# One more entry in a placer's table: a transfer that depends on an earlier transfer of the same queue

## Chip, cores and metric

One core of one Trainium2 chip. The metric is the device time of one execution of the whole program in microseconds (us).

## What is computed

One layer of a hybrid backbone: 512 latent tokens and a prefix of 256 context tokens, model width 2048. A conditioning vector makes shift, scale and gate; the normalised tokens go through one input projection (`u = h @ w_in`, 8 kinds of 1024 columns each and some gate columns); half of the columns feed a bidirectional gated DeltaNet with 8 heads of 128, the other half a bidirectional RWKV-7 with 16 heads of 64; both branches are normalised, gated, and go through one output projection and a final RMSNorm. The part that matters here is the chunk of 64 tokens:

```python
lmat = jnp.where(strict, jnp.einsum('bhncd,bhnsd->bhncs', kb, k) * decay, 0.0)
tmat = lax.linalg.triangular_solve(eye + lmat, jnp.broadcast_to(eye, lmat.shape),
                                   left_side=True, lower=True, unit_diagonal=True)
u = tmat @ (v * beta[..., None])
wk = tmat @ (kb * jnp.exp(g)[..., None])
...
def step(state, inp):
    u_i, wk_i, attn_i, q_i, k_i, gl_i = inp
    v_new = u_i - wk_i @ state
    o_i = q_i @ state + attn_i @ v_new
    state = state * jnp.exp(gl_i)[..., None, None] + jnp.einsum('bhcd,bhce->bhde', k_i, v_new)
    return state, o_i
```

Every chunk of every head needs the inverse of a unit triangular 64x64 matrix before the scan over chunks can start.

## The kernel before

**Stages.** The work is cut into 16 mixers. Mixers 0 to 7 are the context mixers (one DeltaNet head and two RWKV heads each, 256 tokens); mixers 8 to 15 are the latent mixers (512 tokens), which start from the states that the context mixers left. The front stage (to about 150 us) makes the normalised tokens. In the context stage TensorE runs the input projection of kinds `Gk`, `Gv`, `Rk`, `Rv` for both token sets, and the context mixers run beside it. Then come the other projections (512 latent tokens alone) beside latent mixers 8 to 10, which share one set of buffers (a lane); latent mixers 11 to 15 alternate between two lanes, beside the four passes of the output projection. Weights come as 128x512 pieces: a load `wr`, a rounding to `wh` on ScalarE, a remainder `wl` on VectorE, and then three products per 128x128 block (`accl<-hhi,wh`, `hlo,wh`, `hhi,wl`; with the context columns also three on `accc`).

**A mixer.** `prep_*` and `blocks` fill the tile `Z` (`Z<-br`). `send` (line 976) stores the 32x32 diagonal blocks of `Z` into the DRAM buffer `DA` with eight transfers. `solve` (line 985) loads `DA` into `solNL`, inverts all blocks at once with 60 short VectorE operations (`solT<-solNL`, `solNL<-solNL,solT`) and stores the result and its transpose into the DRAM buffer `DD`. `levels` (line 1005) loads `DD` back, with four transfers into `lt` and eight into `Z`, and puts the 32x32 blocks together to 64x64 with two bundles of small products (`wm<-lt,Z` and `pss<-Z,lt`). `chain` (line 1044) is the scan over chunks, `outp` the gated normalisation. So each mixer holds two places where a transfer reads what an earlier one wrote: `DA` (store, then load) and `DD` (store, then loads). All transfers are issued by SP, in the order in which the program lists them.

PSUM tiles have in the trace the name of the first tile in their slot: `wm`, `pss` and `br` are work banks, `accl` and `accc` accumulators of the projections. `Gk` and `t` stand for several SBUF tiles of one slot, `gw` and `ks` are GpSimd's inputs (the gate weights, and the sums behind a key's norm).

**What sets the order.** The kernel records all operations (`record`, line 352), and a list scheduler, the placer (`schedule`, line 450), sets in which order each engine gets them; line 705 issues them, so nearly every row of the profile shows that line. The placer keeps a clock per engine and gives each engine the operation that is ready and of the highest rank. An operation becomes ready when its predecessors are done, plus a latency from two tables: `LAT` for two engines, `OWN` for one (line 396), with -1 where nothing is to be waited for:

```python
            if a.eng == eng:
                lat = OWN.get(eng, -1) if sync else -1
...
                c.ready = max(c.ready, (s if lat < 0 else fin + lat))
```

With -1 the dependent may be placed from the predecessor's start `s`, else from its end `fin`. For a transfer, `s` is the start of its issue on SP, and the placer's `fin` is its own idea of the landing (475 ns of issue, 650 ns, the bytes over 360 per ns, 900 ns). The order only: the real waits are semaphores, and are there whatever the placer thinks. Where the placer sees TensorE without work it puts in fill products (`wm<-zero`).

Of the kernel before, what the change touches and what calls it, by code (L numbers as in the profile page):

```python
# [85 lines left out]
def layout(inp):  # L86
# [22 lines left out]
    def put(n, a):  # L109
# [36 lines left out]
LAT = {"VV": 127, "VA": 128, "VG": 155, "VT": 149, "VS": 110, "AV": 142, "AA": 140, "AG": 125, "AT": 164, "AS": 110,  # L146
       "GG": 97, "GV": 60, "GA": 75, "GT": 120, "GS": 110, "TV": 196, "TA": 197, "TG": 224, "TS": 200,
       "ST": 2000, "SV": 600, "SA": 600, "SG": 600}
OWN = {"V": 120, "A": 148, "G": 107}
EXTRA = {"V": 93, "A": 70, "G": 48, "T": 50, "S": 50, "P": 0}  # L150
HAM, WARM = 10240 / 3, 3060

# [128 lines left out]
class Rec:  # L281
# [70 lines left out]
    def record(self, eng, fn, args, kw):  # L352
# [41 lines left out]
        for a, sync in preds.items():  # L394
            if a.eng == eng:
                lat = OWN.get(eng, -1) if sync else -1
            else:
# [1544 lines left out]
```

## Time and profile before

| | |
|---|---|
| time, median of 3 runs | 2160.66 us (2158.78 to 2163.45) |
| the profiled execution | 2166.2 us, its span 2164.4 us |
| TensorE busy | 1966.3 us (91%) |
| VectorE busy | 1475.2 us (68%) |
| ScalarE, GpSimd busy | 815.9 us (38%), 640.2 us (30%) |

The span is from the first to the last instruction; 1.8 us of the profiled execution's time lie around it. TensorE's busy share is no measure of its useful work: products overlap, their ends are modelled, and fill products count.

### The profile page before, as it was taken

What the parts mean: (1) busy time and instruction counts of PE and PEld (TensorE: products, weight loads), DVE (VectorE), ACT (ScalarE), POOL (GpSimd) and SP (SyncE); (2) the same over time, 40 slices, a digit from 0 to 9 for tenths busy, and PEclk for the clock granted to TensorE, in tenths of its full rate; (3) what the DMA queues carried; (4) which work ended last, traced back from release to release, by engine and by line L of the source; (5) the groups of instructions that cost most, each with busy time, mean ns of one, the idle gap of its engine ahead of it and who ended that gap; (6) DMA issues with size and microseconds to landing.
All of it is one profiled execution on the core that took longest, in us unless ns stands there. A gap on an engine that the chain in (4) does not pass through costs nothing.

```text
span 2164.4 us, 44432 instructions
## 1 busy us (share of the span) xinstructions
PE 1966.3 (91%) x16999; PEld 1542.0 (71%) x17000; DVE 1475.2 (68%) x3397; ACT 815.9 (38%) x2127; POOL 640.2 (30%) x799
## 2 busy tenths in 40 slices
PE   7999999999999999999999999978887897889877
PEld 5678887777877778776777777756665666667666
DVE  6436578675867769574765865786868577767747
ACT  4443333333242433324434434436424452435235
POOL 0003404213140421101212202235823564246226
PEclk8999999999999999999999999999979899899998
DMA  8964433333333333344541542544631544044702
GB/s 305 358 221 109 114 92 95 94 89 88 95 98 90 103 101 88 84 114 124 143 133 47 157 128 67 177 140 143 202 87 44 150 154 136 24 123 123 229 12 97
DMA packets 230517, 269.33 MB, mean 124 GB/s; under 512 B 117280, under 2 KB 130080, under 8 KB 226208
## 3 DMA queue, kind: packets, MB, share of 16 engines
q1 hardware_dynamic: 230304, 266.49, 41.8%
q8 instruction: 133, 2.18, 0.4%
q14 instruction: 80, 0.66, 0.1%
HBM read 210.50 MB, written 55.89 MB: 123 GB/s over the span
## 4 chain that ended last, share of the span: by engine, by line
PE 51%; DVE 22%; DMA 12%; issue 5%; SPq 5%; ACT 3%; POOL 3%; DVEq 0%; ACTq 0%; POOLq 0%
PE accl L705 23%; PE wm L705 8%; PE pss L705 7%; PE br L705 7%; PE accc L705 6%; DVE solNL L705 6%; SPq L705 5%; DVE solT L705 4%; DMA DD<-solNL 3%; DVE Gk L705 3%; DVE wl L705 2%; DMA DA<-Z 1%; DVE t L705 1%; DMA solNL<-DA 1%; DMA yl<-yd 1%
## 5 line engine op out<-in xcount | busy, mean ns | idle before, releaser
L705 ACT ACTIVATE wh<-wr 128x512 fp32r<-128x512 f32 x312 | 196.1, 629 | 375.5 <-PE accc L705 144.3
L705 PE MATMUL accl<-hhi,wl 128*128 128x512 f32 x768 | 317.1, 413 | 10.9 <-DVE wl L705 10.9
L705 PE MATMUL accl<-hhi,wh 128*128 128x512 f32 x768 | 314.1, 409 | 1.8 <-issue 1.8
L705 PE MATMUL accl<-hlo,wh 128*128 128x512 f32 x768 | 312.7, 407 | 0.0
L705 DVE TENSOR_TENSOR wl<-wr,wh 128x512 fp32r<-128x512 f32 x264 | 187.6, 713 | 106.9 <-ACT wh L705 102.5
L705 PE MATMUL accl<-yh,wh 128*128 128x512 f32 x480 | 199.3, 418 | 22.0 <-ACT yh L705 13.8
L705 PE MATMUL accl<-yl,wh 128*128 128x512 f32 x480 | 198.7, 414 | 0.1
L705 PE MATMUL accl<-yh,wl 128*128 128x512 f32 x480 | 197.1, 412 | 1.5 <-DVE wl L705 0.9
L705 PEld LDWEIGHTS accl<-hhi,wl 128*128 128x128 f32 x768 | 146.9, 191 | 50.9 <-DVE wl L705 13.3
L705 DVE TENSOR_TENSOR solNL<-solNL,solT 48x30 f32<-48x30 f32 (+29 forms) x480 | 175.2, 365 | 10.3
L705 DVE TENSOR_TENSOR solT<-solNL 48x30 f32<-48x30 f32 (+29 forms) x480 | 170.6, 355 | 9.0
L705 POOL TENSOR_TENSOR SRd<-Sbd,Dd 64x128 f32<-64x128 f32 x160 | 71.1, 444 | 354.2 <-DVE Sbd L705 348.1
L705 PE MATMUL wm<-zero 128*128 128x128 bf16 x1846 | 146.2, 232 | 30.3 <-DVE SG L705 15.0
L705 PEld LDWEIGHTS accl<-hhi,wh 128*128 128x128 f32 x768 | 146.9, 191 | 20.6 <-issue 4.3
L705 PEld LDWEIGHTS accl<-hlo,wh 128*128 128x128 f32 x768 | 147.0, 191 | 20.2 <-issue 3.2
L705 PEld LDWEIGHTS <-zero 128*128 128x128 bf16 x1864 | 124.4, 105 | 51.7 <-issue 46.6
L705 PE MATMUL accc<-clo,wh 128*128 128x256 f32 x512 | 149.9, 293 | 0.0
L705 PE MATMUL accc<-chi,wh 128*128 128x256 f32 x512 | 147.6, 288 | 0.0
L705 PE MATMUL accc<-chi,wl 128*128 128x256 f32 x512 | 145.9, 285 | 0.0
L705 PEld LDWEIGHTS accl<-yh,wh 128*128 128x128 f32 x480 | 90.9, 191 | 43.2 <-ACT yh L705 15.0
L705 PEld LDWEIGHTS accc<-clo,wh 128*128 128x128 f32 x512 | 97.3, 190 | 24.1 <-issue 0.9
L705 PEld LDWEIGHTS accc<-chi,wh 128*128 128x128 f32 x512 | 97.3, 190 | 21.5 <-issue 0.7
(312 smaller groups left out, 4207.8 us busy)
## 6 DMA issues: line engine op xcount, KB each, us to landing
wr<-win SPq DMA_DIRECT2D x256, 256.0 KB, 3.2
wa<-wada SPq DMA_DIRECT2D x32, 1024.0 KB, 6.0
ud<-Gk SPq DMA_DIRECT2D x72, 256.0 KB, 2.6
gw<-wada SPq DMA_DIRECT2D x64, 256.0 KB, 3.5
wr<-wout SPq DMA_DIRECT2D x64, 256.0 KB, 2.9
Rk<-ud SPq DMA_DIRECT2D x48, 256.0 KB, 3.2
rtd<-xt SPq DMA_DIRECT2D x48, 256.0 KB, 2.2
xr<-rtd SPq DMA_DIRECT2D x32, 256.0 KB, 3.0
```

The lines of the kernel that those rows point to most:

```text
L705: r = getattr(self.engs[o.eng], o.fn)(*args, **kw)
```

## The change

`OWN` gets an entry for transfers. A transfer that depends on an earlier one is now ready 1500 ns after the placer's landing of the earlier one, and no longer at the start of its issue. Nothing else is edited; no operation, tile or buffer is added or removed, apart from the fill products that the placer puts in itself.

```diff
 LAT = {"VV": 127, "VA": 128, "VG": 155, "VT": 149, "VS": 110, "AV": 142, "AA": 140, "AG": 125, "AT": 164, "AS": 110,
        "GG": 97, "GV": 60, "GA": 75, "GT": 120, "GS": 110, "TV": 196, "TA": 197, "TG": 224, "TS": 200,
        "ST": 2000, "SV": 600, "SA": 600, "SG": 600}
-OWN = {"V": 120, "A": 148, "G": 107}
+OWN = {"V": 120, "A": 148, "G": 107, "S": 1500}
```

The order of all engines changes. On SP, around the second context mixer's second hop, before:

```order
L705 DMA wr_0_1430<-win 128x512
L705 DMA DD_1_116<-solNL_1424 48x2x1024
L705 DMA lt_0_2052<-DD_1_116 32x6x32
L705 DMA Z_1_2025<-DD_1_116 32x6x32 x2
...
L705 DMA ud_110<-Gk_1_1443 128x512
L705 DMA wr_1_1431<-win 128x512
L705 DMA wr_2_1432<-win 128x512
L705 DMA gw_0_1453<-wada 128x512
L705 DMA gw_2_1455<-wada 128x512
```

and now:

```order
L705 DMA wr_1_1431<-win 128x512
L705 DMA DD_1_116<-solNL_1424 48x2x1024
L705 DMA gw_0_1453<-wada 128x512
L705 DMA gw_2_1455<-wada 128x512
L705 DMA ud_110<-Gk_1_1443 128x512
L705 DMA wr_2_1432<-win 128x512
L705 DMA lt_0_2052<-DD_1_116 32x6x32
L705 DMA Z_1_2025<-DD_1_116 32x6x32 x2
```

Two gate weight loads, a store of projected columns and a weight load went from behind the twelve loads of `levels` to between the store of `DD` and these loads. In all 16 mixers nothing stood between that store and the first load; now one to six transfers do, 56 in all. Between the last store of `DA` and the load of `solNL` nothing stood either; now there are none in the last mixer and 1 to 14 in the others, 47 in all.

On VectorE, around the start of the same mixer's solution (`solNL` in the first row of type `TENSOR_SCALAR`), before:

```order
L705 COPY R_329_0_2054<-Vtok_1_2049 64x128 x2
L705 TENSOR_SCALAR solNL_1424<-solNL_1424,cst_60 48x1024
L705 TENSOR_TENSOR wl_2_1438<-wr_2_1432,wh_2_1435 128x512
L705 SCALAR_TENSOR_TENSOR solNL_1424<-solNL_1424,cst_60 48x1024
L705 TENSOR_TENSOR dg_0_2029<-dg_0_2029,Gc_0_91 128x256
L705 TENSOR_TENSOR solT_1425<-solNL_1424 48x30
L705 TENSOR_TENSOR dg_0_2029<-dg_0_2029,cst_60 128x256
```

and now:

```order
L705 COPY R_329_0_2054<-Vtok_1_2049 64x128 x2
L705 TENSOR_TENSOR wl_2_1438<-wr_2_1432,wh_2_1435 128x512
L705 TENSOR_TENSOR dg_0_2029<-dg_0_2029,Gc_0_91 128x256
L705 TENSOR_TENSOR dg_0_2029<-dg_0_2029,cst_60 128x256
L705 TENSOR_SCALAR solNL_1424<-solNL_1424,cst_60 48x1024
```

A remainder of weights (`wl`) and two operations of the next mixer (`dg`) went ahead of the first operation that needs the load of `solNL`.

On TensorE the order is told in counts. The 512-column products of the projections that stand ahead of the first bundle of `levels` are 11 to 29 more for context mixers 0 to 6, 21 more for mixer 7, 56 and 107 more for mixers 8 and 9, and 192 more (with 154 more fill products) for mixer 10; in mixers 11, 13 and 15 they differ by -6, 0 and -31. Fill products are 1994 in all, 1846 before.

## Rows read from the trace of the kernel before

**Rows 1.** The profiler's page: the span, and busy time by engine with its share of the span and the count of instructions.

```profile
span 2164.4 us, 44432 instructions
...
PE 1966.3 (91%) x16999; PEld 1542.0 (71%) x17000; DVE 1475.2 (68%) x3397; ACT 815.9 (38%) x2127; POOL 640.2 (30%) x799
```

**Rows 2.** Busy time of each engine by stretch (start:end in us from the span's start, its length, then busy us and, in brackets, instructions of each engine; then the granted clock of TensorE as a share of full speed, the DMA engines' busy share, and GB/s).

```profile
150.00:1000.00 850.00, 811.52 (x6042) 658.22 (x6041) 600.08 (x1459) 282.20 (x736) 216.24 (x264) 0.98 0.36 97
1000.00:1380.00 380.00, 365.68 (x2722) 279.29 (x2722) 251.98 (x554) 155.09 (x406) 73.64 (x113) 0.99 0.44 123
1380.00:1470.00 90.00, 70.99 (x692) 55.06 (x692) 70.67 (x150) 36.98 (x102) 25.69 (x32) 0.94 0.56 161
1380.00:2164.00 784.00, 652.02 (x7018) 507.39 (x7016) 553.69 (x1239) 319.25 (x886) 347.62 (x412) 0.92 0.41 121
```

**Rows 3.** The SP queue's own waits over the whole span (what was waited for: us in total, times, longest us).

```profile
SPq L705 <- POOL gw L705: 128.0, 37, 8.8
...
SPq L705 <- DMA DD<-solNL: 60.0, 16, 4.7
...
SPq L705 <- DMA DA<-Z: 32.6, 18, 3.8
```

**Rows 4.** Waits in the context stage, 150 to 1000 us, of TensorE and then of VectorE (us in total, times, longest us).

```profile
PE accl L705 <- DVE wl L705: 10.9, 6, 3.2
PE wm L705 <- DMA lt<-DD: 9.6, 10, 1.6
PE br L705 <- DVE t L705: 7.7, 4, 3.4
...
DVE solNL L705 <- DMA solNL<-DA: 16.8, 7, 4.6
```

**Rows 5.** The same waits later: TensorE from 1000 to 1380 us, TensorE from 1380 us to the end, VectorE from 1380 us to the end.

```profile
PE wm L705 <- DMA lt<-DD: 3.2, 3, 1.2
...
PE wm L705 <- DMA lt<-DD: 16.1, 13, 2.6
...
DVE solNL L705 <- DMA solNL<-DA: 10.0, 4, 3.8
```

**Rows 6.** DMA issues over the span (count, KB each, median us from issue to landing); then two rows on `DD` alone: its sixteen stores (ns of one issue, then the start of the first and of the last in us), and us from issue to landing of all transfers that touch it (minimum, median, maximum).

```profile
DD<-solNL SPq DMA_DIRECT2D x8, 768.0 KB, 4.3
...
DA<-Z SPq DMA_DIRECT2D x64, 48.0 KB, 2.3
...
L705 SPq DMA_DIRECT2D DD<-solNL x16: 305/332/339, 306.9 to 2035.5; - x16
...
DMA to landing us min/median/max: 1.6/2.0/5.1
```

**Rows 7.** Instructions in order of time around the second context mixer's first hop (start us, us, engine, line, operation, result <- inputs, count, and in brackets the idle time before it with what ended it): SP, then VectorE.

```profile
355.80 0.79 SPq L705 DMA_DIRECT2D DA<-Z  x2
358.94 0.31 SPq L705 DMA_DIRECT2D solNL<-DA  x1
...
356.05 1.32 DVE L705 COPY R<-Vtok 64x128 f32<-64x128 f32 x2 [0.94 <-ACT Vtok L705]
361.94 0.74 DVE L705 TENSOR_SCALAR solNL<-solNL,cst 48x1024 f32<-48x1024 f32 x1 [4.57 <-DMA solNL<-DA]
362.61 0.68 DVE L705 TENSOR_TENSOR wl<-wr,wh 128x512 fp32r<-128x512 f32 x1
...
365.23 0.40 DVE L705 TENSOR_TENSOR dg<-dg,Gc 128x256 f32<-128x256 f32 x1
```

**Rows 8.** The same mixer's second hop, in the same columns: SP, GpSimd (POOL), VectorE, TensorE.

```profile
396.59 0.33 SPq L705 DMA_DIRECT2D DD<-solNL  x1
400.34 0.33 SPq L705 DMA_DIRECT2D lt<-DD  x1
...
407.86 1.94 SPq L705 DMA_DIRECT2D gw<-wada  x2
...
412.43 1.05 POOL L705 TENSOR_TENSOR gw<-gw,scT 128x512 f32<-128x512 f32 x1 [9.72 <-DMA gw<-wada]
...
416.15 0.42 DVE L705 TENSOR_TENSOR t<-br,ks 128x256 f32<-128x256 f32 x1 [5.81 <-POOL ks L705]
...
401.21 0.40 PE L705 MATMUL accl<-hhi,wh 128*128 128x512 f32 x1
401.44 0.39 PE L705 MATMUL accl<-hlo,wh 128*128 128x512 f32 x1
...
402.26 0.40 PE L705 MATMUL accl<-hhi,wh 128*128 128x512 f32 x1
...
406.64 0.57 PE L705 MATMUL wm<-lt,Z 32*32 32x32 f32 x42 [0.84 <-DMA lt<-DD]
...
416.63 0.69 PE L705 MATMUL br<-cst,t 128*128 128x128 f32 x2 [3.41 <-DVE t L705]
```

**Rows 9.** The fourth latent mixer's second hop, in the last stage: SP, then TensorE.

```profile
1583.12 0.30 SPq L705 DMA_DIRECT2D DD<-solNL  x1
...
1593.52 0.41 SPq L705 DMA_DIRECT2D Rk<-ud  x1
...
1582.51 3.46 PE L705 MATMUL wm<-zero 128*128 128x128 bf16 x56
...
1594.10 1.48 PE L705 MATMUL wm<-lt,Z 32*32 32x32 f32 x90 [1.28 <-DMA lt<-DD]
```

## Prediction

> **What bounds the kernel now.** I read the page first, then the table of stretches, then who waits for whom in each stretch, and last single hops in the order of time. The page has TensorE at 91% [rows 1], but that says little here; the stretches say more. From 150 to 1380 us TensorE is busy 811.5 of 850 and 365.7 of 380 us at a granted clock of 0.98 and 0.99 [rows 2]: projections are always at hand, and time is lost only where TensorE, which works in order, stands at an operation whose input is late. From 1380 us on it is 652 of 784 us, a good part of it fill products, and VectorE is at 553.7 (71%): the two lanes of mixers set the pace there, and TensorE waits for them.
>
> Next, what a hop costs. SP stands 60.0 us over 16 times for the landing of a `DD` store, and 32.6 us over 18 times for that of a `DA` store [rows 3]. It stands there because the placer thinks that the dependent transfer can follow at once. The landing takes 4.3 us for the large `DD` store and 2.3 us for the large `DA` stores [rows 6]. While SP stands, what is queued behind it stands too, and the engines that were told to expect the data stand at it.
>
> The second context mixer shows both hops. First hop: the last `DA` store is issued in the row that starts at 355.80, SP reaches the load at 358.94, and VectorE, put in front of it since the end of `R` at 357.37, is idle 4.57 us until 361.94 [rows 7]. Second hop: `DD` at 396.59, first load back at 400.34; TensorE waits 0.84 us in the middle of its bundle at 406.64. Two gate weight loads leave SP only from 407.86; GpSimd is idle 9.72 us for them, the sum `ks` is queued behind on GpSimd, VectorE waits 5.81 us for `ks`, and TensorE 3.41 us for `t` at 416.63 [rows 8]. So one hop is paid for at three places.
>
> **The change part by part.** It removes no hop: the landings stay as long as they are. What can go is the standing of engines that have other work. I count it by stage, in TensorE's own waits where TensorE is the bound.
>
> *Context stage.* TensorE waits 9.6 us for `lt`, 10.9 us for `wl` and 7.7 us for `t` [rows 4], 28.2 us together.
> - The `lt` waits are ten, the longest 1.6 us. In the new order 11 to 29 more projection products of 512 columns stand ahead of the first bundle in mixers 0 to 6. Three of them and their three of 256 columns take 402.26 - 401.21 = 1.05 us [rows 8], so the least is 11/3 x 1.05 = 3.9 us, more than any of these waits. I take all: -9.6. (Bounds 0 and -9.6.)
> - The `wl` waits follow VectorE's idle time at `solNL`, 16.8 us in seven waits [rows 4]. In the hop shown, the new order puts a `wl` (0.68) and two `dg` operations (0.40 each) ahead of the solution: 1.5 us of the 4.57 us [rows 7]. VectorE has little else that is ready, so I take a third: -3.6. (Bounds 0 and -10.9.)
> - The `t` waits come by way of the gate weights. Two of those loads now stand ahead of the twelve loads of `levels`, but they wait for their own buffers too. I take half: -3.8. (Bounds 0 and -7.7.)
>
> Sum: -17.0.
>
> *One lane, 1000 to 1380 us.* The `lt` waits are 3.2 us [rows 5], and 56 and 107 products more stand ahead of the bundles there: -3.2.
>
> *Last stage.* TensorE waits 16.1 us for `lt` in 13 waits, VectorE 10.0 us for the load of `DA` [rows 5]. In the fourth latent mixer the store is issued at 1583.12, and the next lane's load of `Rk` leaves only at 1593.52; TensorE stands 1.28 us at 1594.10 with nothing else that it may do [rows 9]. Work of the other lane can fill such a hole, but a lane whose own hop is the end of the chain gains nothing. I take half of the first and a third of the second: -8.0 - 3.3 = -11.3. (Bounds 0 and -26.1.)
>
> *What is added.* 148 fill products: 56 of them took 3.46 us [rows 9], 0.062 each, so 9.2 us if all lay on the path; the placer puts them where it sees TensorE idle, half of which I count: +4.6. The 56 + 47 transfers put into the hops cost an issue of some 0.3 to 0.4 us each [rows 7, 8], four of them 1.6 us, which fits in a landing of 2.3 to 4.3 us: nothing, if none of them waits for something itself. And the 1.5 us stand on top of a landing that the placer already counts (for the 768 KB of `DD` its figures give 4.2 us against 4.3 measured [rows 6]), so it brings each mixer's next step later than needed. Mixer 7, after which the latent mixers start, has 21 products more ahead: 21 x (401.44 - 401.21) = 4.8 us [rows 8], of which I take 2: work is moved there, not added.
>
> Sum: -17.0 - 3.2 - 11.3 + 4.6 + 2.0 = -24.9 us on a span of 2164.4 us: 2139.5, with the 1.8 us around it 2141.3. The profiled execution, 2166.2, is 5.5 us above the median of the three runs, so against that median: 2160.66 - 24.9 = **2136 us**. A change below 0.2% (4.3 us) can't be told from none here. The bounds of the waits (-57.5 us if all go, about +14 us if none goes and all additions count) give 2103 to 2175.
>
> **The rivals.**
>
> *The chain of mixers sets the end, and is made later: slower.* For it: the extra 1.5 us come twice in each mixer, and the delay adds up: 56, 107, 192 products more ahead of mixers 8, 9 and 10. Mixer 10's bundle stands behind 192 x 0.23 = 44.2 us (the same spacing) and 154 x 0.062 = 9.5 us more. TensorE had 90 - 71 = 19.0 us to spare where mixer 10 ran (1380 to 1470 us [rows 2]), and the 20.2 us saved before it count against it: 44.2 + 9.5 - 19.0 - 20.2 = +14.5, 2175 us. Against it: mixers 11, 13 and 15, the lane that ends last, have -6, 0 and -31 products more ahead, so the delay is not handed on. It decides where the last `DD` store, at 2035.5 us before [rows 6], comes later than that. Chance 0.13.
>
> *A transfer that is put into the hop waits itself.* SP stands 128.0 us over 37 times for GpSimd to free a `gw` buffer, 3.5 us each and up to 8.8 [rows 3], and just such loads now stand between `DD` and its loads back. Where one waits longer than the landing, the loads of `levels` are late, and the three context gains shrink by some 10 us: 2146 us. Against it: the 3.9 us and more of products ahead of the bundle cover part of it. Beside it, by the Trainium skill ("DMA: Bandwidth & Descriptors", section "Issuing engines are not separate DMA queues"), all transfers run on the same 16 engines and interleave, so that what is put into a hop would also lengthen it. Here the loads back take 2.0 us in the middle and 5.1 at most [rows 6], so by that rule up to 3.1 us more per mixer, less than the 3.9 us put ahead; the engines are at 0.36 in this stage [rows 2]. No row of the kernel before shows a hop with weight loads inside it. Chance 0.15.
>
> *More than that.* SP is free for up to 92.6 us more [rows 3], and the other lane's loads come earlier in the last stage, where every late load is on a chain. If all waits counted above go and the additions hide, 2160.66 - 57.5 = 2103 us. Against it: VectorE shows little ready work at the first hop. Chance 0.17.
>
> *Nothing.* The waits go, but the two lanes after 1380 us start from the same point and VectorE, at 71% there with waits on products between, takes back what was won: 2161 us. Chance 0.10.
>
> **How the numbers follow.** The forecast itself has 0.45, with a range of its own of 2122 to 2150. Cut at 2108, which leaves out half of the case with more gain (0.09), and at 2168, which leaves out most of the slower one (0.11): the range 2108 to 2168 holds 0.80. Faster by over 0.2%: 0.45 + 0.17 + 0.12 of the waiting transfers = 0.74. Within 0.2%: 0.10 and 0.02 = 0.12. Slower: 0.13 and 0.01 = 0.14.
>
> **What would show it.** Right: SP's waits for `DD` and `DA` fall to a fraction of 92.6 us; TensorE's waits for `lt` in the context stage to nearly none, those for `wl` by a third and for `t` by half; the context stage, where the first two stores of `DD` lie 396.59 - 306.9 = 89.7 us apart [rows 6, 8], ends about 15 us earlier. Half right: these fall, and the last store is no earlier than 2035.5 us. Wrong: SP waits for `gw` between `DD` and `lt`, or the last store is later than before. If the time comes out well below 2108 us, the last stage gained more than the context stage, and the price of a blocked SP was put too low; above 2168 us, the mixers' chain was the bound all along.

## The result, and the profile after

The changed kernel takes 2106.19 us (median; 2101.0 to 2108.05) where the kernel before took 2162.05 us beside it: a ratio of 0.9735, 95% interval 0.9706 to 0.9763. That is 56 us, where 25 were forecast, and 2 us below the range. The direction was right, and in the context stage the waits that were named; the size was not.

The page of the profiled execution (2107.17 us): span, busy time by engine, and TensorE's granted clock in 40 slices. It answers [rows 1].

```profile
span 2105.4 us, 44731 instructions
...
PE 1945.2 (92%) x17147; PEld 1529.5 (73%) x17148; DVE 1482.5 (70%) x3397; ACT 818.9 (39%) x2127; POOL 646.7 (31%) x799
...
PEclk8999999999999999999999999999889999999998
```

Busy time by stretch, in the columns of [rows 2]:

```profile
150.00:1000.00 850.00, 834.59 (x6216) 678.48 (x6216) 615.88 (x1494) 301.04 (x788) 221.79 (x272) 1.00 0.39 105
1000.00:1380.00 380.00, 370.24 (x2795) 283.15 (x2793) 263.45 (x573) 160.95 (x409) 78.19 (x116) 0.99 0.46 130
1380.00:2105.00 725.00, 603.66 (x6918) 471.06 (x6916) 533.86 (x1185) 297.89 (x829) 344.06 (x401) 0.95 0.41 118
```

TensorE is busy 834.6 of 850 us in the context stage instead of 811.5, and its granted clock is 1.00 instead of 0.98. In the last stage the clock is 0.95 instead of 0.92.

SP's own waits (us in total, times, longest us), against [rows 3]:

```profile
SPq L705 <- POOL gw L705: 97.1, 30, 6.9
...
SPq L705 <- DMA DD<-solNL: 11.2, 10, 3.1
SPq L705 <- DMA DA<-Z: 9.7, 7, 2.6
```

The large stores of `DD` (count, KB each, median us from issue to landing), then all sixteen, and us from issue to landing of all transfers that touch it, against [rows 6]:

```profile
DD<-solNL SPq DMA_DIRECT2D x8, 768.0 KB, 5.3
...
L705 SPq DMA_DIRECT2D DD<-solNL x16: 304/332/382, 306.6 to 1975.9; - x16
...
DMA to landing us min/median/max: 1.6/2.1/7.2
```

SP stands 20.9 us for the two landings instead of 92.6. The last `DD` store is issued at 1975.9 us instead of 2035.5. The large stores land in 5.3 us where it was 4.3; the longest landing, 7.2 us, is that of the last store (before, 5.1 us, that of the store at 1271.0).

Waits in the context stage, of TensorE and then of VectorE, against [rows 4]:

```profile
PE br L705 <- DVE t L705: 5.2, 6, 1.6
PE accl L705 <- DVE wl L705: 4.6, 3, 3.0
...
DVE t L705 <- POOL ks L705: 22.2, 7, 4.3
...
DVE solNL L705 <- DMA solNL<-DA: 5.7, 4, 3.4
```

TensorE has no wait for `lt` left there (9.6 before).

The second context mixer's second hop now, on SP, and the first operation on `t` behind it on TensorE (start, us, engine, and so on), against [rows 8]:

```profile
394.22 0.34 SPq L705 DMA_DIRECT2D DD<-solNL  x1
394.61 2.36 SPq L705 DMA_DIRECT2D gw<-wada  x2
397.07 0.39 SPq L705 DMA_DIRECT2D ud<-Gk  x1
397.55 0.38 SPq L705 DMA_DIRECT2D wr<-win  x1
398.17 0.33 SPq L705 DMA_DIRECT2D lt<-DD  x1
...
406.74 0.44 PE L705 MATMUL br<-cst,t 128*128 128x128 f32 x2 [0.77 <-DVE t L705]
```

The two gate weight loads leave at 394.6, 13 us earlier than at 407.86; four transfers fill the landing, `lt` follows at 398.17, 4.0 us behind the store (3.75 before), and the wait of 3.41 us for `t` is 0.77 us.

### The profile page after: what moved, and what is told of

It is laid out like the page before. It is cut to its first block, busy times and chain, and to the rows that moved or that the text cites. A ratio compares the mean times of both kernels' runs of the same rounds, so it can differ in the third digit from the quotient of the medians.

```text
span 2105.4 us, 44731 instructions
## 1 busy us (share of the span) xinstructions
PE 1945.2 (92%) x17147; PEld 1529.5 (73%) x17148; DVE 1482.5 (70%) x3397; ACT 818.9 (39%) x2127; POOL 646.7 (31%) x799
## 5 line engine op out<-in xcount | busy, mean ns | idle before, releaser
L705 PE MATMUL wm<-zero 128*128 128x128 bf16 x1994 | 159.0, 234 | 29.8 <-DVE SG L705 11.4
L705 PEld LDWEIGHTS <-zero 128*128 128x128 bf16 x2012 | 137.1, 106 | 53.8 <-issue 48.7
L705 PEld LDWEIGHTS accl<-yh,wh 128*128 128x128 f32 x480 | 90.4, 189 | 42.8 <-ACT xt L705 11.5
```

Source lines behind the costliest of these rows:

```text
L705: r = getattr(self.engs[o.eng], o.fn)(*args, **kw)
```

## Where the 59 us of the span went

The `DD` stores of the sixteen mixers (0 to 15) cut the span. Between store 0 and store 7 lies the context stage, from 9 to 15 the last stage.

| us | before | after | difference |
|---|---|---|---|
| start to store 0 | 306.9 | 306.6 | -0.3 |
| 0 to 7 (context) | 651.7 | 621.0 | -30.7 |
| 7 to 9 (one lane) | 312.4 | 312.3 | -0.1 |
| 9 to 15 (last stage) | 764.5 | 736.0 | -28.5 |
| 15 to the end | 128.9 | 129.5 | +0.6 |

The same cuts as stretches, in the columns of [rows 2]. Context stage before, then after:

```profile
306.90:958.60 651.70, 620.34 (x4784) 501.03 (x4786) 473.31 (x1173) 217.04 (x576) 164.69 (x198) 0.98 0.36 95
```

```profile
306.60:927.60 621.00, 608.96 (x4779) 493.21 (x4779) 471.62 (x1173) 217.50 (x576) 165.33 (x198) 1.00 0.37 100
```

All but five of its products are there again. TensorE is idle 12.0 us instead of 31.4: 19.3 us less. And it is busy 11.4 us less with the same work; nearly all of that is the clock, as the next slices show. The two add up to 30.7 us.

Where the clock fell before is seen in slices of 1 us: at 414 to 422, 517 to 525, 605 to 613, 670 to 675 and 763 to 767 us, each with 1.7 or 3.4 us of full-speed time lost, 13.6 us together. Of these, 1.3 us lie inside the waits, where nothing ran; 12.3 us fall on work. After, one stretch is left, at 643 to 648 us, with 1.7 us on work. So the clock gave back 10.6 of the 11.4 us. The waits of TensorE behind which it fell in the kernel before (last column), and two behind which it did not (374.40 and 474.26):

```profile
374.40 0.50 PE L705 MATMUL accl<-hhi,wl 128*128 128x512 f32 x1 [2.36 <-DVE wl L705]
...
416.63 0.69 PE L705 MATMUL br<-cst,t 128*128 128x128 f32 x2 [3.41 <-DVE t L705]
...
474.26 0.50 PE L705 MATMUL accl<-hhi,wl 128*128 128x512 f32 x1 [2.19 <-DVE wl L705]
...
516.84 0.44 PE L705 MATMUL br<-cst,t 128*128 128x128 f32 x2 [3.12 <-DVE t L705]
...
605.82 0.24 PE L705 MATMUL wm<-lt,Z 32*32 32x32 f32 x2 [1.63 <-DMA lt<-DD]
606.91 0.84 PE L705 MATMUL wm<-lt,Z 32*32 32x32 f32 x42 [0.85 <-DMA lt<-DD]
...
669.31 0.50 PE L705 MATMUL accl<-hhi,wl 128*128 128x512 f32 x1 [3.21 <-DVE wl L705]
...
762.92 0.76 PE L705 MATMUL accl<-hhi,wl 128*128 128x512 f32 x1 [1.98 <-DVE wl L705]
```

And the first of them in slices of 2 us (TensorE's busy us, then the granted clock):

```profile
412.00:414.00 2.00, 1.21 (x15) 1.00 0.57 205
414.00:416.00 2.00, 0.00 (x0) 0.71 0.00 0
416.00:418.00 2.00, 1.37 (x4) 0.50 0.55 139
418.00:420.00 2.00, 2.00 (x14) 0.50 0.15 43
420.00:422.00 2.00, 2.00 (x8) 0.59 0.36 88
422.00:424.00 2.00, 2.00 (x23) 1.00 0.00 0
```

TensorE stands 3.41 us, and after it has data again it runs at 1.2 GHz, half of 2.4, until nearly 422 us. So the wait costs its length, and then half of the time that TensorE works at the low level: here some 5 us, so 2.5 us. The Trainium skill ("TensorE: Matmul & The Clock Gate", section "HAM oscillation — how this bites in real kernels") tells the same of a kernel that waits some 3 to 5 us for each piece of data: after the wait the clock is throttled, and the throttled time costs half its length. The trace agrees, with 2.5 us lost behind a wait of 3.41, and the rows above have the same behind shorter waits.

The last stage in the same way, before and after:

```profile
1271.00:2035.50 764.50, 659.00 (x6785) 501.75 (x6784) 543.60 (x1226) 309.99 (x856) 322.06 (x392) 0.93 0.44 129
```

```profile
1239.90:1975.90 736.00, 631.80 (x6874) 483.81 (x6872) 539.82 (x1205) 302.82 (x842) 327.21 (x392) 0.95 0.44 126
```

Here TensorE's idle time is the same (105.5 and 104.2 us); it is busy 27.2 us less. But it is not the bound here, so that is no proof of a cause. The experiments below take it up.

## The experiments

All times are ratios to the kernel before on the same chip. The parts are the stretches of the table above, each read from the one execution that was profiled. Executions of one program differ: 25 of the kernel before, beside x_jitter_v, took 2145.7 to 2178.9 us. "Hop" is the pair of a store to `DA` or `DD` and the load that reads it back.

| kernel | context | last stage | ratio (95%) |
|---|---|---|---|
| before | 651.7 | 764.5 | 1 |
| changed kernel | 621.0 | 736.0 | 0.9735 (0.9706 to 0.9763) |
| x_sp_back | 681.0 | 772.4 | 1.0267 (1.0224 to 1.0311) |
| x_sp_forward | 679.3 | 761.5 | 1.0118 (1.0067 to 1.017) |
| x_context | 620.7 | 748.3 | 0.9793 (0.975 to 0.9836) |
| x_latent | 652.8 | 784.4 | 1.0135 (1.0085 to 1.0186) |
| x_dd | 623.2 | 771.1 | 0.9932 (0.9898 to 0.9966) |
| x_da | 630.4 | 768.6 | 1.0023 (1.0 to 1.0047) |
| x_rest | 654.2 | 747.4 | 0.9954 (0.9929 to 0.9979) |
| x_margin0 | 615.4 | 751.9 | 0.977 (0.9737 to 0.9803) |
| x_margin750 | 614.4 | 768.9 | 0.9833 (0.9781 to 0.9885) |
| x_margin1400 | 617.3 | 739.0 | 0.9717 (0.9686 to 0.9748) |
| x_margin1600 | 616.1 | 738.5 | 0.9725 (0.9692 to 0.9758) |
| x_margin3000 | 623.4 | 746.9 | 0.985 (0.9817 to 0.9884) |
| x_jitter_v | 653.8 | 758.0 | 0.9995 (0.9962 to 1.0028) |
| x_jitter_g | 647.6 | 756.4 | 0.995 (0.9922 to 0.9978) |
| x_jitter_a | 649.5 | 762.7 | 1.0 (0.9973 to 1.0028) |
| x_hold_ctx | 646.7 | 758.4 | 0.9936 (0.9906 to 0.9966) |
| x_hold_all | 644.7 | 753.3 | 0.9912 (0.9882 to 0.9943) |
| x_hold_after | 618.9 | 735.9 | 0.9728 (0.9701 to 0.9755) |

### SP's order or that of the engines?

Two kernels take one without the other: the changed kernel's order on the compute engines with the loads of the hops put back, and the kernel before with these loads moved forward on SP alone.

```diff
+    def moved(self, order, back):
+        hops = [o for o in seq if o.eng == "S" and isinstance(o.args[1], View) and o.args[1].t.key[:2] in ("DA", "DD")]
...
-            self.rec.emit(order)
+            self.rec.emit(self.rec.moved(order, True))
```

> The changed kernel with the order of TensorE, VectorE, ScalarE and GpSimd untouched, but on SP the loads that read DA or DD stand again right behind the last store, so SP stands at each landing as before the change. Theory A (the gain is that the four computing engines are told to expect the data later): SP stands some 90 us again and the time stays near the changed kernel's 2106 us, at most 10 us more. Theory B (the gain is that SP is no longer blocked, so that the other transfers leave earlier): at least half of the 56 us is lost, 2134 us or more.

Measured: 2224.31 us, by the two ratios 5.5% above the changed kernel. SP's waits are back, and TensorE and VectorE stand in the context stage at what comes by way of the gate weights:

```profile
SPq L727 <- DMA DD<-solNL: 62.9, 16, 5.8
SPq L727 <- DMA DA<-Z: 29.5, 20, 3.0
...
PE br L727 <- DVE t L727: 43.0, 5, 9.9
...
DVE t L727 <- POOL ks L727: 63.9, 7, 13.2
```

The kernel before gets the same function with loads moved forward past up to three other transfers:

> The kernel before with the order of the four computing engines untouched, but on SP the loads that read DA or DD go behind up to three of the transfers that follow them. Theory A: no gain, 2155 to 2168 us, since VectorE and TensorE still stand at the hop. Theory B: SP's waits for DA and DD fall to under 30 us and at least half of the gain is there, 2134 us or less.

Measured: 2194.14 us. SP waits only 2.7 us for `DD` and 11.2 us for `DA`, but the engines, in the order of before, expect the data at once:

```profile
PE wm L730 <- DMA lt<-DD: 26.0, 31, 2.6
PE accl L730 <- DVE wl L730: 19.7, 8, 5.3
...
DVE solNL L730 <- DMA solNL<-DA: 29.2, 8, 5.0
```

Both theories fall as single causes. Freeing SP alone is worse than standing, and so are the new compute orders alone. What pays is that the two fit: SP fills the landing, and the engines' orders know that the data comes later. This rests on one way of taking each without the other; no second way was run.

### Which mixers, which hop

The number is taken into account only for some of the pairs; here for those of the context mixers (their buffers are `DA0` and `DD0`):

```diff
                 lat = OWN.get(eng, -1) if sync else -1
+                hop = {t.key[:3] for t in a.tiles if t in o.tiles}
+                if eng == "S" and not hop & {"DA0", "DD0"}:
+                    lat = -1
```

> The new latency only for the DA and DD of the eight context mixers. Theory A, and that the stages add up: by the last context mixer's DD store the 31 us of the changed kernel are there, and nothing is won after it: about 2131 us. Theory C (any reshuffling of the list would move the time by tens of us, and this one was lucky): the time has no relation to the stage, somewhere from 2110 to 2180 us, and the events of the last stage drift by more than 15 us against those of the kernel before moved by 31 us.

Measured: 2120.91 us, with the whole gain of the context stage (620.7 us) and 16 us of the last stage's.

> The new latency only for the DA and DD of the eight latent mixers. Theory A with added stages: the context stage is the kernel before's to 1 us, and some 28 us are won after 1380 us: about 2134 us. Theory C: no relation, from 2110 to 2180 us.

 (The test is `hop & {"DA1", "DD1"}`.)

Measured: 2196.08 us, slower, and outside what either theory allowed. The context stage is that of before, the last stage 20 us longer. So the parts don't add: alone, the hops of the latent mixers cost time; on top of the context hops, together with the other dependent transfers, they come with a gain of 12 us.

> The landing is counted only where the dependent loads read back `DD` (the second hop of each mixer, 4.3 us); loads of `DA` follow at once, as in the kernel before. Theory A (the second hop carries the context gain, since its late loads hold up `lt`, the gate weights and `t`): last `DD` store of mixer 7 some 20 to 25 us earlier than before, of the 31 us that the whole change gave; SP's wait for `DA` stays near 30 us. Theory B (the first hop carries it, through `solNL`, `wl` and the order around them): mixer 7 less than 10 us earlier. Theory C (after 1380 us the time depends on the order as a whole and no part has a price of its own): whatever mixer 7 shows, the end may be anywhere from 30 us earlier to 30 us later than before. Time by A without C: 2169 - 40 = some 2130 us; by B: about 2160 us.

 (The test is `{t.key[:2] ...} & {"DD"}`.)

Measured: 2145.57 us. The context stage is 28.5 us shorter, though SP still waits 33.9 us for `DA`.

> The landing is counted only where the dependent loads read back `DA` (the first hop, 2.3 us). Theory A: mixer 7 less than 10 us earlier, SP's wait for `DD` stays near 60 us, time about 2160 us. Theory B: mixer 7 20 us and more earlier, time about 2130 us. If the two hops add up, the gains at mixer 7 in this run and in that with `DD` alone sum to some 31 us; if the sum is far smaller, the hops only pay together; if far larger, either order alone already takes the gain. Theory C as for the run with `DD` alone: the end is open by some 30 us to either side.

 (The test is `& {"DA"}`.)

Measured: 2164.92 us. The context stage is 21.3 us shorter, though SP waits 64.2 us for `DD` and TensorE's waits for `lt` there are as before:

```profile
PE wm L708 <- DMA lt<-DD: 9.2, 11, 1.6
PE accl L708 <- DVE wl L708: 4.9, 5, 1.6
```

Neither A nor B alone: each hop takes most of the 30.7 us, 49.8 in sum. What the two kernels have in common is that between stores 0 and 7 TensorE's idle time is down to 13.2 and 16.5 us, and only one stretch at half clock is left, with 1.7 us lost. And both give a part of it, or all, back later: their last stages are 6.6 and 4.1 us longer than before, and mixers 8 and 9 cost x_da 11.5 us more.

> The landing is counted only for transfers of SP that depend on each other in other ways than by `DA` and `DD`. The kernel's order parts from that of before only in the last third of the program. Both theories: context stage as before within 3 us, and SP's waits for `DD` and `DA` near 60 and 33 us. Without theory C the time is within 6 us of before; by theory C up to 35 us to either side.

 (The test is `hop - {"DA", "DD"}`.)

Measured: 2151.47 us, 0.46% faster than before, with SP's waits for `DD` at 56.9 and for `DA` at 32.0 us. The context stage is as before (654.2), the last stage 17 us shorter: an order that counts neither hop can gain as much there. But the change's entry counts these other pairs too, among them the stores to `ud` and `yd` and the loads that read them back, and the prediction has no term for them. SP's own waits for `ud` and `yd` fell by only 5.4 us, from 12.2; whether the 17 us come of these landings, of the order or of the spread of executions was not separated.

### Is it only a redrawn order?

```diff
-OWN = {"V": 120, "A": 148, "G": 107}
+OWN = {"V": 122, "A": 148, "G": 107}
```

> The kernel before, without any counting of a landing, and one figure of the placer changed by 2 ns: VectorE's wait for its own earlier result 122 instead of 120. Its orders part from those of before in the second context mixer, and no transfer stands in a hop, as before. Theory D (the context stage of the kernel before is an unlucky order, and nearly any other would gain, since each hop alone took some 25 to 31 us): the last `DD` store of mixer 7 is 15 us and more earlier than before. Theory H (the gain comes of putting work into the hops): mixer 7 within 8 us of before. By theory C (after 1380 us any change of the order moves the end) the time is 2161 with up to 35 us to either side; if instead the end has a price by parts, it is within 10 us of before.

> As the run before, with GpSimd's figure 109 instead of 107 ns; the orders part from those of before in the middle of the context stage. Theory D: mixer 7 earlier than before by 5 us and more. Theory H: within 5 us. Theory C: the end up to 35 us to either side of before; without it within 10 us.

> The kernel before with ScalarE's figure 150 instead of 148 ns, a third redrawn order without hops; it parts from the order of before only at the end of the context stage. From mixer 9 to mixer 15 (before 764.5, the other redrawn orders 758.0, 756.4 and, with the landing counted for other transfers, 747.4 us): 750 to 772 us if the hops carry a gain of their own; below 745 us would say that the draw alone gives it. Time 2145 to 2172 us.

Measured: 2162.56, 2156.41 and 2162.37 us. In the context stage 653.8, 647.6 and 649.5 us against 651.7: theory D is not borne out, though on two draws only. TensorE's order parts from that of before at 424 us in x_jitter_v and at 803 us in x_jitter_g; in x_jitter_a it does so behind the stage. With one hop or both counted for the context mixers that stage took 614.4 to 630.4 us in nine kernels (x_context has the changed kernel's order there), without them 647.6 to 654.2 in six. Four of these six, before, x_latent, x_rest and x_jitter_a, have the same order in that stage, so their 649.5 to 654.2 us are the spread of executions. In the last stage the three are 2 to 8 us shorter than before. But x_hold_ctx (below), with the order of before there, is 6 us shorter too, so this shows no effect of the order.

### The margin

```diff
-OWN = {"V": 120, "A": 148, "G": 107, "S": 1500}
+OWN = {"V": 120, "A": 148, "G": 107, "S": 0}
```

> As the changed kernel, but with 0 instead of 1500 ns on top of the landing that the placer already counts. If the context gain comes from other work being put into the landing, mixer 7 is earlier than before by 25 to 35 us here too, since the placer's own figure for the landing (4.2 us against 4.3 measured) already holds it; SP's waits for `DD` and `DA` stay below a third of 92.6 us, but above the 20.9 us of the changed kernel. If the extra 1.5 us carry it (the true end of a hop is later than the landing), mixer 7 gains only some 15 us. By theory C the end differs from the changed kernel by tens of us either way although the context stage is the same: 2090 to 2160 us.

> As the changed kernel, with 750 instead of 1500 ns on top of the landing. Counted from mixer 9's last `DD` store to mixer 15's (764.5 us in the kernel before; 736.0, 751.8, 738.9, 746.9 us with margins of 1500, 0, 1400 and 3000). If the hops carry a gain in the last stage: 753 us or less here, the time 2099 to 2118 us. If it is the draw of the order alone: anywhere from 736 to 775 us. Mixer 7 in both cases 921 to 934 us.

> As the changed kernel, with 1400 instead of 1500 ns on top of the landing. Theory H: mixer 7 within 6 us of the changed kernel. Theory C: the end moves by more than 8 us although nothing in the hops is different; if the time instead follows the margin smoothly (0 ns gave 2109.0, 1500 gave 2106.2, 3000 gave 2127.0 us), it is 2103 to 2110 us.

> As the run before, with 1600 ns: from mixer 9 to mixer 15 at most 753 us and the time 2099 to 2118 us if the hops carry a gain in the last stage; 736 to 775 us, the time up to 2145 us, if it is the draw of the order.

> As the changed kernel, but with 3000 instead of 1500 ns. Context stage: the placer brings each next step another 1.5 us later, twice in each mixer; if that delay is paid, mixer 7 is later than in the changed kernel by up to 8 x 3 = 24 us; if it is covered by projections, within 4 us of it. SP's waits for `DD` and `DA` fall below 20.9 us. Fill products are 181 more than in the changed kernel, 0.062 us each, so up to 11 us. By theory C the end is again open by tens of us: 2095 to 2170 us.

Measured: 2109.0, 2127.19, 2104.38, 2105.07 and 2126.95 us. The margin is not what matters: with 0 ns the context stage is shorter than with 1500 (615.4 against 621.0), so the figure for the landing itself is enough. SP's waits in that kernel are 28.8 us for `DD` and 10.6 for `DA`, 43% of the 92.6 us before, where a third had been expected at most. The last stage does not follow the margin: 751.9, 768.9, 739.0, 736.0, 738.5, 746.9 us from 0 to 3000. With 750 ns that stage is 16 us longer than a gain carried by the hops would allow, with 1600 it lies inside. The first does not decide: the four executions with 750 ns took 2117.7, 2118.4, 2136.0 and 2136.6 us, and the longest is the one that was profiled.

### The clock by itself

The orders of the kernel before stay as they are, on SP too; ahead of the products at which TensorE waited, fill products are put in by position.

```diff
+HOLES = {
+    2210: 33, 2468: 50, 2648: 17, 2764: 30, 2946: 19, 3020: 45, 3508: 21, 3872: 46, 4039: 11, 4427: 27,
+    5112: 14, 5576: 12, 5631: 36,
+}
...
+            if o.eng == "T":
+                out += [(s, self.warm.clone()) for _ in range(HOLES.get(k, 0))]
+                k += 1
```

> The kernel before, with the orders of all engines and of SP untouched, and 361 fill products put ahead of the 13 products at which TensorE waited 1.0 us and more between 350 and 985 us (26.7 us of waits; a product takes 0.062 us at the full clock, and each wait is filled up to 0.3 us short of its length). TensorE is busy while it waits, no transfer stands in a hop. Theory K (a long wait costs twice: its length, and then a stretch of 3.4 to 6.8 us at half the clock behind it): the half-clock stretches of the context stage (13.6 us of clock lost between 400 and 770 us, by slices of 1 us) go, and the last `DD` store of mixer 7 is 9 to 14 us earlier than 958.6; the time 10 to 15 us below before. Theory W (only the waits themselves cost, the clock's fall lies in time that is lost anyway): mixer 7 within 3 us of before, or later by the fills' own waits, and the time within 5 us of before.

Measured: 2151.47 us, 0.64% below before (0.34 to 0.94%). The wait of [rows 8] is now filled (TensorE's instructions in order of time):

```profile
409.51 3.10 PE L719 MATMUL wm<-zero 128*128 128x128 bf16 x50
413.31 0.44 PE L719 MATMUL br<-cst,t 128*128 128x128 f32 x2 [0.69 <-DVE t L719]
```

And the clock does not fall behind it (slices of 2 us, then the context stage):

```profile
414.00:416.00 2.00, 2.00 (x19) 1.00 0.10 39
416.00:418.00 2.00, 2.00 (x23) 1.00 0.51 131
418.00:420.00 2.00, 2.00 (x21) 1.00 0.42 112
...
303.30:950.00 646.70, 632.56 (x5098) 515.13 (x5099) 468.12 (x1173) 216.59 (x576) 163.80 (x198) 0.99 0.35 96
```

314 of the stage's products are the fills, 19.5 us at 0.062; the rest takes 613.1 us instead of 620.3: 7.2 us less. The half clock that falls on work went from 12.3 to 5.1 us, by the same 7.2. Idle time and fills together are 33.6 us, 2.2 more than the idle time of before. So the stage is 5.0 us shorter, and the store of mixer 7 comes 8.6 us earlier, of which 3.6 lie ahead of the first store. Theory K is borne out in kind; of the 9 to 14 us expected, the stage itself shows 5.0. It is 2.8 us below the shortest of the four executions without fills, and the next kernel repeats it.

> As the run before, with 1203 fill products ahead of the 46 products at which TensorE waited 1.0 us and more between 350 and 2120 us (89.8 us of waits). Theory K, if TensorE's clock counts after 1380 us as in the context stage: granted clock of the whole from 0.955 to above 0.97, the time 25 to 40 us below before. If the lanes' chains over VectorE set the end there, the clock rises and the time gains no more than the context stage gave (10 to 15 us). Theory W: within 5 us of before.

Measured: 2145.63 us. The context stage, with the same order and the same fills as the run before:

```profile
307.10:951.80 644.70, 632.88 (x5099) 515.59 (x5100) 469.25 (x1173) 216.84 (x576) 166.12 (x198) 0.99 0.33 96
```

So the two executions with fills took 646.7 and 644.7 us, the four without 649.5 to 654.2: 6.4 us between the means. The clock of the whole rises from 0.955 to 0.978, above that of the changed kernel, and the time gains 0.88%, not 2.7%. The last stage is 753.3 us, against 764.5 and 758.4 in two executions of that order without fills there. After 1380 us the clock sets little of the end.

> The changed kernel with 687 fill products ahead of the 28 products at which TensorE waited 1.0 us and more in its own trace between 350 and 2060 us (51.9 us of waits). Theory K: the clock from 0.973 to some 0.985, mixer 7 within 3 us of the changed kernel (only one stretch of 1.7 us is left there), the time 5 to 20 us below it, 2086 to 2101 us. Theory W: within 5 us of the changed kernel, or slower.

Measured: 2106.27 us, that of the changed kernel. Its two stages, in the columns of [rows 2]:

```profile
306.10:925.00 618.90, 610.56 (x4832) 494.96 (x4831) 472.15 (x1173) 217.16 (x576) 164.56 (x198) 1.00 0.35 100
1236.60:1972.50 735.90, 651.64 (x7413) 506.93 (x7412) 524.36 (x1205) 302.69 (x842) 328.84 (x392) 0.97 0.44 126
```

The clock of the last stage is 0.97 instead of 0.95, its length 735.9 us instead of 736.0. There the 5 to 20 us of theory K were wrong.

## Why the prediction was wrong in size

**What bounds the kernel.** Right as to the stages. But the granted clock of 0.98 in [rows 2] was quoted and not priced: 0.02 of 850 us is 17 us (15.3 in slices of 1 us from 150 to 960), more than any of TensorE's waits on the list. In a stage that TensorE bounds such a column is a term of the sum. The span fell by 34.1 us more than the 24.9 of the sum: 13.7 in the context stage, 17.2 in the last stage and 6.6 for additions that were not seen, with 3.1 less in the one lane and 0.3 less at the two ends.

**Context stage.** Forecast -17.0, measured -30.7. TensorE's idle time fell by 19.3, so the waits were sized well as a sum, not one by one: `lt` went from 9.6 to none as forecast, `wl` from 10.9 to 4.6 (a third was taken, more than half went), `t` from 7.7 to 5.2 (half was taken, a third went). That `lt` counted most is not borne out: with its waits left in place (x_da) the stage still gained 21.3 us. **The step that failed** is a term put at nothing without a reason: the half-clock time behind those waits. TensorE's busy time fell by 11.4 us, 10.6 of them by the slices at half clock. The direct test of it took 7.2 us off the busy time, for 7.2 us of half clock on work that went.

**One lane.** Forecast -3.2, measured -0.1.

**Last stage.** Forecast -11.3, measured -28.5. The waits named there did go: TensorE's for `lt` from 16.1 to 1.1 us, VectorE's for the load of `DA` from 10.0 us to none. **This step failed too**, as a term mis-sized by 17.2 us, and its cause stays open. Filling TensorE's waits here (x_hold_after) left the stage at 735.9 us, so a share of those waits is no price for it. Six margins with all hops counted gave 736.0 to 768.9 us, 746.9 on average; five orders without hops 747.4 to 764.5, 757.8 on average. The means differ by 10.9 us, close to the term forecast, but with ranges that overlap and a counterexample in x_latent. The changed kernel has the shortest of the six, 10.9 us below their mean. Margins of 1400, 1500 and 1600 ns, whose orders differ from the context stage on, agree within 3.0 us, so it is not the luck of one order alone. That the hops as such gain anything in this stage, and how much, stays open, and so does what the other dependent transfers and the order give.

**What is added.** Forecast +6.6 (fills and mixer 7). Mixer 7 is not later but 31 us earlier, and the fills cannot be seen: 687 more of them, put into TensorE's waits (x_hold_after), changed nothing. So fills that lie in waits cost no time that shows; whether all those of the placer lie there was not looked at.

**The rivals.** The chain of mixers made later: it does appear at mixer 10, whose store moves from 1447.0 to 1462.2 us, 15 us later (14.5 were worked out there), but it is not handed on, as the argument against it said; the last store is 59.6 us earlier. Transfers that wait inside the hop: SP's waits for `gw` fell from 128.0 to 97.1 us. The first load from `DD` comes 3.9 to 5.2 us behind its store in the context mixers (3.7 to 3.9 before) and 4.6 to 7.3 us in the latent ones (4.3 to 5.1). By the Trainium skill ("DMA: Bandwidth & Descriptors", section "Issuing engines are not separate DMA queues") all transfers run on the same 16 engines and interleave. What is put into the hop does lengthen it here: the large stores land in 5.3 us instead of 4.3, and in 4.3 again in x_sp_back, where the loads follow them at once. The loads back hardly changed in the middle (2.1 us instead of 2.0); their longest is 5.9 us instead of 4.0. The prediction took 5.1 us for the longest of these loads, but that was a store. None of this kept the context stage from gaining 30.7 us. "More than that" gave 2103 us by all listed waits going; the time is there within 3 us, but by another sum: some waits stayed, and the clock and the last stage made up for them. The sign named for a time below 2108 us, that the last stage gained more than the context stage, does not hold: 28.5 against 30.7 us. "Nothing" fell.

## What to carry to other kernels

Where an in-order TensorE is the bound, a wait is priced at its length and, if the clock falls behind it, at half of the work time at the low level: read the granted clock stage by stage and turn its distance from 1 into us before any other term. A placer that takes an in-order queue's dependent transfer to follow at once harms two things together, what stands behind it on the queue and what the engines are told to expect; correcting one without the other was slower here than correcting neither (+58 and +25 us). And where chains on several engines set the end, re-run the placer with a figure changed by 2 ns, and the same program several times, before calling a gain of 1% of that stage the effect of an edit: three such draws moved the time by 0 to 0.5%, and two executions of one order differed by 6 us in the last stage.

## What the runs showed of the hardware beyond what was expected

The clock fell behind waits as short as 1.63 us (605.82, with a second one of 0.85 us right after it) and 1.98 us (762.92), and did not fall behind waits of 2.36 and 2.19 us (374.40 and 474.26). So the length of a wait alone does not tell whether the clock falls. A full-length fill with cheap products (50 of them, 3.10 us) kept it at 1.00 with the same late data behind it. The large `DD` stores landed later when other transfers were issued right behind them: 5.3 us in the changed kernel and 5.7 with 3000 ns, against 4.3 before and in x_sp_back.
